# Streaming the 264 token columns of every matmul as two halves in turn, in a one-layer hybrid decoder step

## The chip, the cores and the metric

One Trainium2 chip, one of its cores. The metric is the device time of one execution in microseconds; the time of a kernel is the median of its runs. TensorE (PE) multiplies, with its weight loads shown as an engine of their own (PEld); VectorE (DVE), ScalarE (ACT) and GpSimd (POOL) work on SBUF and PSUM; SyncE (SP) issues most of the DMAs.

## The reference

One step of a decoder layer for 256 prompt tokens and 8 sample tokens, 264 tokens in all, width 2048, all in float32:

```python
def layer(x, ...):
    xn = rmsnorm(x, g_mix)
    z = xn @ w_in                                   # 2048 x 5128
    xr, conv_new = causal_conv(z[..., OFF_RGX:OFF_RGG], conv_buf, conv_w, conv_b)
    ...                                             # RG-LRU over xr, gated by gelu
    y_rg = rmsnorm((h_rg.astype(dt) * jax.nn.gelu(z[..., OFF_RGG:OFF_Q])), g_rg_out)
    ...                                             # q, k, v, gates of the mLSTM
    h_ml, C_new, n_new, m_new = mlstm(q, k, v, logi, logf, C0, n0, m0)
    y_ml = h_ml * jax.nn.sigmoid(z[..., OFF_O:OFF_I])
    x = x + jnp.concatenate([y_rg, y_ml], axis=-1) @ w_out
    xq = (rmsnorm(x, g_xa) @ w_xa_q).reshape(B, L, XA_HEADS, XA_DH)
    ...                                             # softmax attention over 256 memory tokens
    x = x + o @ w_xa_o
    xf = rmsnorm(x, g_ffn)
    x = x + (jax.nn.silu(xf @ w_ffn_gate) * (xf @ w_ffn_up)) @ w_ffn_down
```

The layer ends with a last RMSNorm, and the new states and the memory keys and values are outputs too.

## The kernel before, in words

Activations are held transposed: the model dimension lies on the 128 partitions in 16 chunks (`KC`), and the 264 tokens (`N`; the first 256, `T`, are the prompt, the last 8 the samples) lie along the free dimension. So the weights are the stationary operand of a matmul (128 x 128) and the tokens the moving one (128 x 264).

To keep float32 accuracy in the fast one-pass format `F32R`, both operands are split into a high part and a low part (`HL` holds such pairs in tiles of the pool `B`, four chunks of 264 columns to a tile). `mm3` makes three matmuls of one product, high x high, high x low and low x high, all of which accumulate in one PSUM bank. A projection step (`proj`) does this for all 16 chunks of the model dimension, 48 matmuls, and leaves 128 output channels x 264 tokens in a bank. `pe_if` does the same for the gate columns with two matmuls a chunk.

A table `steps` lists the weight pieces in their order: the combined input projection (41 pieces), the output projection (16), the queries (16), memory keys and values, the attention's output (16), then for three parts of the feed-forward width the gate and up pieces in turn, each followed by the 16 pieces of the down projection. For each step the main loop starts the load of a later piece on SP's queue, lets ACT and DVE split the next piece into its halves (a tile `w`), issues the matmuls, and hands the bank to an evacuation function (`evac_...`, `residual`, `final`) that is emitted one step later. Side work (recurrences, attention, norms) is cut into generators that a pump places between the steps by a price model. Inside this, the Tile scheduler orders instructions by a simulated timeline, and only SP's order is kept as written.

The evacuation functions read the bank from PSUM on DVE (or ACT) with the tokens in order, mostly as `ps[:, :N]`, multiply by the row of inverse norms `rstd` or add to the residual `xres`. Two of them part the prompt columns from the 8 sample columns: `evac_rgx` writes the prompt part into a row with three leading zeros and each sample behind its own three history values, and `evac_q` writes the samples into `qsm`. `final(15)` reads the last output tile in two pieces so that DVE and ACT follow each other sooner.

Matmuls that are not of 264 columns (memory keys and values, attention, sums over tokens, the broadcast of norms) and the plain-float matmuls of the RG gates in `rg_gen` don't go through `mm3` with a 264-column bank.

Line 60 of the profile is the wrapper `Engine`, through which all compute instructions of PE, DVE and ACT are called, so the profile's groups are told apart by tile names: `mm` and `ax` are PSUM banks, `w` split weights, `raw` loaded weights, `B` the general pool, `t` temporaries.

Of the kernel before, what the change touches and what calls it, by code (L numbers as in the profile page):

```python
# [13 lines left out]
AF = mybir.ActivationFunctionType  # L14
OP = mybir.AluOpType
AX = mybir.AxisListType

P = 128
D = 2048
KC = D // P  # L20
T = 256
NS = 8
N = T + NS
# [6 lines left out]
KSCALE = 128.0 ** -0.5  # L30
# [50 lines left out]
def layer_kernel(ctx: ExitStack, tc, xT, memT, vec, wrg, w_in, w_out, w_q, w_k, w_v, w_o,  # L81
# [3 lines left out]
    act, dve, pe = Engine(nc.scalar, price_act), Engine(nc.vector, price_dve), Engine(nc.tensor, price_pe)  # L85
# [18 lines left out]
    def B(shape, dt=F32):  # L104
        return sb.tile(shape, dt, tag="B", bufs=NB, name=nm("B"))

    def tmp(w=N, tag="t"):
        t = sb.tile([P, N], F32, tag=tag, bufs=NT if tag == "t" else NL, name=nm(tag))
        return t[:, :w]
# [109 lines left out]
    class W:  # L219
# [3 lines left out]
        def __call__(self, c, w=P):  # L223
# [5 lines left out]
            o = (c % per) * w  # L229
            return wh[:, o: o + w], wl[:, o: o + w]  # L230

    def mm3(ps, a, b, start, stop):
        ah, al = a
        bh, bl = b
        pe.matmul(ps, ah, bh, start=start, stop=False)
        pe.matmul(ps, ah, bl, start=False, stop=False)
        pe.matmul(ps, al, bh, start=False, stop=stop)
# [20 lines left out]
    def side(g, prio=0):  # L258
        x = Gen(g, prio)
        gens.append(x)  # L260
        gens.sort(key=lambda q: q.prio)
        return x
# [12 lines left out]
    def finish(cond):  # L275

        for _ in range(10000):
            if cond():
                return
            pump(1e12)  # L280
        raise RuntimeError("side work does not end")
# [6 lines left out]
    def bank(tag="mm"):  # L288
        return psm.tile([P, 512], F32, tag=tag, bufs=4, name=nm(tag))
# [16 lines left out]
    def V(name, j=0, w=1):  # L306
        o = _V[name][0] + j
        return vecs[:, o: o + w]
# [52 lines left out]
    def sumsq(acc, x, first):  # L361
        if first:
            return act.activation(acc, x, AF.Square)
        s = tmp(x.shape[-1])
        i = act.activation(s, x, AF.Square)
        dve.tensor_add(acc, acc, s)
        return i
# [29 lines left out]
    rstd = const.tile([P, N], F32, name="rstd")  # L397
# [48 lines left out]
    def evac_rgx(n):  # L446
        def f(ps):
            if n == 0:
                rg["xr"] = Arr(RGB)
            z = B([P, 2, 292])  # L450
            zi = z[:, 0, :]
            dve.memset(zi[:, 0:3], 0.0)
            smp = zi[:, 259:291].rearrange("p (b j) -> p b j", j=4)
            hist = V("cst", n * 24, 24).rearrange("p (b j) -> p b j", j=3)
            act.activation(smp[:, :, 0:3], hist, AF.Copy)
            dve.tensor_mul(zi[:, 3:259], ps[:, :T], rstd[:, :T])
            dve.tensor_mul(smp[:, :, 3:4], ps[:, T:N].rearrange("p (b j) -> p b j", j=1),
                           rstd[:, T:N].rearrange("p (b j) -> p b j", j=1))
            rg["z", n] = z
            rg["zn"] = n + 1  # L460
        return f
# [67 lines left out]
    def evac_rgg(n):  # L529
        def f(ps):  # L530
            z = tmp()
            dve.tensor_mul(z, ps[:, :N], rstd)
            act.activation(z, z, AF.Gelu_apprx_tanh)
            h = rg["h"](n)
            dve.tensor_mul(h, h, z)
            sumsq(acc_rg, h, n == 0)
            if n == RGB - 1:
                st["rgout"] = side(rg_out(), 0)
        return f
# [13 lines left out]
    ml = {}  # L553
# [12 lines left out]
    def pe_if(i):  # L566
        ps = bank()
        for c in range(KC):
            w = splits[i, c // 8][:, c % 8, :]
            xh, xl = rx(c)  # L570
            pe.matmul(ps[:, :N], w, xh, start=c == 0, stop=False)
            pe.matmul(ps[:, :N], w, xl, start=False, stop=c == KC - 1)
        return ps

    def evac_if(ps):
        R = Arr(7)
        ml["R"] = R
        li, u, a, b = (R(j)[0:4] for j in range(4))
        act.activation(a, ps[64:68, :N], AF.Copy)
        act.activation(b, ps[96:100, :N], AF.Copy)  # L580
        dve.tensor_add(li, ps[0:4, :N], a)
        dve.tensor_add(u, ps[32:36, :N], b)
        dve.tensor_mul(li, li, rstd[0:4, :])
        dve.tensor_mul(u, u, rstd[0:4, :])
        dve.tensor_scalar(li, li, V("bi")[0:4], None, op0=OP.add)
        dve.tensor_scalar(u, u, V("bf")[0:4], None, op0=OP.add)
        ml["gates"] = side(ml_gates(), 1)
# [52 lines left out]
    def evac_qk(j):  # L640
        def f(ps):
            if j == 0:
                ml["qk"] = Arr(8)
            if j < 4:
                dve.tensor_mul(ml["qk"](j), ps[:, :N], rstd)
            else:
                dve.scalar_tensor_tensor(ml["qk"](j), ps[:, :N], KSCALE, rstd, op0=OP.mult, op1=OP.mult)
            if j == 7:
                ml["sg"] = side(ml_sample(), 3)
                side(ml_prompt(), 2)  # L650
                side(ml_values(), 2)
                ml["pg"] = side(ml_heads(), 2)
        return f

    def evac_v(j):
        def f(ps):
            if j == 0:
                ml["v"] = Arr(8)
            dve.tensor_mul(ml["v"](j), ps[:, :N], rstd)
            ml["vn"] = j + 1  # L660
        return f

# [193 lines left out]
    def evac_o(j):  # L856
        def f(ps):
            z = tmp()
            dve.tensor_mul(z, ps[:, :N], rstd)
            act.activation(z, z, AF.Sigmoid)  # L860
            if j == 0:
                st["yml"] = HL(8)
            finish(lambda: ml.get("nn", 0) > j // 2)
            dve.tensor_mul(z, z, hT["t"](j))
            split(*st["yml"](j), z, V("g_ml", j))
        return f
# [45 lines left out]
    def residual(m, gname, key, last):  # L912

        def f(ps):
            x = xres[:, m, :]
            dve.tensor_add(x, x, ps[:, :N])
            if key is None:
                return
            if m == 0:
                st[key] = HL(KC)  # L920
            split(*st[key](m), x, V(gname, m))
            sumsq(acc_x, x, m == 0)
            if m == KC - 1:
                st["rstd_" + key] = side(last(), -1)
        return f
# [4 lines left out]
    def final(m):  # L930

        def f(ps):
            x = xres[:, m, :]
            if m == 0:
                st["y"] = Arr(KC)
            if m < KC - 1:
                dve.tensor_add(x, x, ps[:, :N])
                sumsq(acc_x, x, m == 0)
            else:
                warm(3)  # L940
                sq = tmp()
                with tc.high_priority():
                    for lo, hi in ((0, P), (P, N)):
                        dve.tensor_add(x[:, lo:hi], x[:, lo:hi], ps[:, lo:hi])
                        act.activation(sq[:, lo:hi], x[:, lo:hi], AF.Square)
                fin_sums(fin["sum"], sq, False)
            act.activation(st["y"](m), x, AF.Copy, scale=V("g_final", m))
            if m == 0:
                act.activation(warm_act, acc_x[:, 0:1], AF.Sqrt)
            elif m == KC - 2:  # L950
                fin["sum"] = bank("ax")
                fin_sums(fin["sum"], acc_x, True)
            elif m == KC - 1:
                rstd_fin(fin["sum"])
        return f
# [33 lines left out]
    qn = {"n": 0}  # L989
    qsm = const.tile([P, KC, NS], F32, name="qsm")  # L990
# [3 lines left out]
    def evac_q(j):  # L994
        def f(ps):
            if j == 0:
                qn["t"] = Arr(KC, T)
            dve.tensor_mul(qn["t"](j), ps[:, :T], rstd[:, :T])
            dve.tensor_mul(qsm[:, j, :], ps[:, T:N], rstd[:, T:N])
            qn["n"] = j + 1  # L1000
            if j == 3:
                with tc.issue_after(st["split"].ins):
                    act.activation(onesr, ones, AF.Copy)
                st["dk"] = side(dec_k(), 5)
                st["dv"] = side(dec_v(), 4)
        return f
# [233 lines left out]
    fz = {}  # L1240
# [6 lines left out]
    def evac_up(part, j):  # L1247
        def g(ps):
            if j == 0:
                st["a", part] = HL(FPARTS[part])  # L1250
            a, b = tmp(), tmp()
            dve.tensor_mul(a, fz["g"][:, :N], rstd)
            act.activation(a, a, AF.Silu)
            dve.tensor_mul(b, ps[:, :N], rstd)
            dve.tensor_mul(b, b, a)
            h, l = st["a", part](j)
            act.activation(h, b, AF.Copy)
            dve.tensor_sub(l, b, h.bitcast(F32))
        return g
# [39 lines left out]
    for i, (src, cols, pef, evf, need) in enumerate(steps):  # L1299
# [18 lines left out]
        ps = pef(i)  # L1318
# [133 lines left out]
```

## Time and profile before

| | |
|---|---|
| median of 3 runs | 1552.85 us (1552.31 to 1553.53) |
| span of the profiled execution | 1548.1 us |
| granted TensorE clock | 0.997 |
| PE busy | 1533.5 us (99%) |
| DVE busy | 1055.5 us (68%) |
| ACT busy | 784.0 us (51%) |
| HBM traffic over the span | 209 GB/s |

Busy time is the union of an engine's instructions in one profiled execution; a group's row gives line, engine, operation, written and read tiles, shapes and count, then busy time in us, the mean of one in ns, and the idle time of the engine just before such instructions with what ended it. The chain is the work that ended last, followed back through its releasers.

### The profile page before, as it was taken

What the parts mean: (1) busy time and instruction counts of PE and PEld (TensorE: products, weight loads), DVE (VectorE), ACT (ScalarE), POOL (GpSimd) and SP (SyncE); (2) the same over time, 40 slices, a digit from 0 to 9 for tenths busy, and PEclk for the clock granted to TensorE, in tenths of its full rate; (3) what the DMA queues carried; (4) which work ended last, traced back from release to release, by engine and by line L of the source; (5) the groups of instructions that cost most, each with busy time, mean ns of one, the idle gap of its engine ahead of it and who ended that gap; (6) DMA issues with size and microseconds to landing.
All of it is one profiled execution on the core that took longest, in us unless ns stands there. A gap on an engine that the chain in (4) does not pass through costs nothing.

```text
span 1548.1 us, 30188 instructions
## 1 busy us (share of the span) xinstructions
PE 1533.5 (99%) x12098; PEld 1500.4 (97%) x12098; DVE 1055.5 (68%) x2026; ACT 784.0 (51%) x1255; POOL 123.7 (8%) x190
## 2 busy tenths in 40 slices
PE   9999999999999999999999999999999999999997
PEld 9999999999999888899999999999999999999997
DVE  7886888796699989876665555445555545555554
ACT  7565775665455656555444444333444433444463
POOL 0001210000134333310000000000000000000000
PEclk9999999999999999999999999999999999999999
DMA  9556984547789887855555555555555555555563
GB/s 301 187 164 204 309 288 171 193 158 259 251 294 356 320 296 252 309 181 180 187 177 181 186 181 188 181 185 183 183 185 181 186 183 186 180 188 178 163 181 107
DMA packets 99757, 326.01 MB, mean 211 GB/s; under 512 B 10945, under 2 KB 19825, under 8 KB 99617
## 3 DMA queue, kind: packets, MB, share of 16 engines
q1 hardware_dynamic: 83472, 269.57, 52.1%
q0 software_dynamic: 15136, 53.16, 9.7%
q8 instruction: 94, 1.54, 0.4%
q10 hardware_dynamic: 1008, 1.36, 0.3%
q14 instruction: 47, 0.38, 0.1%
HBM read 312.78 MB, written 11.28 MB: 209 GB/s over the span
## 4 chain that ended last, share of the span: by engine, by line
PE 96%; DVE 2%; ACT 1%; DMA 0%; issue 0%; SPq 0%; DVEq 0%; ACTq 0%
PE mm L60 90%; PE ax L60 6%; DVE B L60 1%; ACT B L60 0%; DVE w L60 0%; DMA raw<-w_in 0%; ACT w L60 0%; ACT L60 0%; DVE xres L60 0%; DVE c L60 0%; ACT rstd L60 0%; SPq L1278 0%; DVE acc_x L60 0%; DVEq L1429 0%; ACT t L60 0%
## 5 line engine op out<-in xcount | busy, mean ns | idle before, releaser
L60 PE MATMUL mm<-B,w 128*128 128x264 f32 (+1 forms) x10960 | 1365.3, 285 | 4.1 <-DVE w L60 2.4
L60 PEld LDWEIGHTS mm<-B,w 128*128 128x128 f32 x10960 | 1338.6, 188 | 16.4 <-DVE w L60 2.8
L60 ACT ACTIVATE w<-raw 128x1024 fp32r<-128x1024 f32 (+1 forms) x522 | 537.9, 1031 | 654.6 <-PE mm L60 447.3
L60 DVE TENSOR_TENSOR w<-raw,w 128x1024 fp32r<-128x1024 f32 (+1 forms) x522 | 623.1, 1195 | 357.0 <-ACT w L60 356.0
L60 PE MATMUL mm<-w,B 128*128 128x512 f32 x384 | 91.0, 391 | 0.0
L60 PEld LDWEIGHTS mm<-w,B 128*128 128x128 f32 x384 | 70.7, 188 | 14.3
L60 DVE TENSOR_TENSOR t<-mm,rstd 128x264 f32<-128x264 f32 x104 | 44.8, 431 | 44.2 <-PE mm L60 43.5
L1344 POOL TENSOR_TENSOR B<-B,rstd 128x264 f32<-128x264 f32 x4 | 2.8, 736 | 855.5 <-ACT rstd L60 855.5
L60 DVE TENSOR_TENSOR xres<-xres,mm 128x264 f32<-128x264 f32 (+1 forms) x81 | 34.2, 423 | 38.9 <-PE mm L60 38.9
L60 DVE SCALAR_TENSOR_TENSOR B<-B,dw 128x256 f32<-128x256 f32 x128 | 55.6, 488 | 3.9 <-ACT dw L60 3.9
L60 DVE SCALAR_TENSOR_TENSOR dw<-B,qsm,dw 128x256 f32<-128x256 f32 x96 | 49.6, 525 | 0.4
L60 PE MATMUL ax<-B,B 128*128 128x256 f32 (+3 forms) x288 | 48.1, 308 | 0.0
L60 PEld LDWEIGHTS ax<-B,B 128*128 128x128 f32 x288 | 40.8, 190 | 3.2 <-ACT w L60 0.3
L1031 POOL TENSOR_TENSOR ds<-dw,ds 128x256 fp32r<-128x256 f32 x32 | 34.6, 1085 | 108.1 <-ACT ds L60 108.1
L60 ACT ACTIVATE B<-xres,vecs 128x264 fp32r<-128x264 f32 (+1 forms) x64 | 32.1, 502 | 1.5 <-DVE xres L60 1.0
L60 ACT ACTIVATE t<-xres 128x264 f32<-128x264 f32 (+2 forms) x61 | 24.0, 410 | 15.2 <-DVE xres L60 15.2
L1020 POOL DMA_DIRECT2D B<-kcT x32 | 17.3, 542 | 140.1 <-DVE B L60 131.0
L60 ACT ACTIVATE B<-t 128x264 fp32r<-128x264 f32 (+1 forms) x60 | 24.2, 409 | 4.6 <-DVE t L60 4.3
L60 DVE TENSOR_TENSOR acc_x<-acc_x,t 128x264 f32<-128x264 f32 x59 | 25.1, 426 | 1.0 <-ACT t L60 0.5
L60 DVE SCALAR_TENSOR_TENSOR B<-xres,vecs,B 128x264 fp32r<-128x264 f32 x48 | 23.4, 487 | 3.1 <-ACT B L60 3.1
L60 ACT ACTIVATE t<-t 128x264 f32<-128x264 f32 (+1 forms) x61 | 24.8, 406 | 1.3 <-DVE t L60 1.2
L60 ACT ACTIVATE dw<-B,qsm 128x256 f32<-128x256 f32 x32 | 16.2, 507 | 17.4 <-DVE B L60 10.7
(152 smaller groups left out, 666.9 us busy)
## 6 DMA issues: line engine op xcount, KB each, us to landing
raw<-w_gu SPq DMA_DIRECT2D x176, 512.0 KB, 3.5
raw<-w_d SPq DMA_DIRECT2D x80, 512.0 KB, 3.5
raw<-w_in SPq DMA_DIRECT2D x74, 512.0 KB, 4.6
raw<-w_out SPq DMA_DIRECT2D x32, 512.0 KB, 4.0
B<-kcT POOLq DMA_DIRECT2D x32, 512.0 KB, 8.1
raw<-w_q SPq DMA_DIRECT2D x32, 512.0 KB, 3.7
B<-vcT POOLq DMA_DIRECT2D x32, 512.0 KB, 8.5
raw<-w_k SPq DMA_DIRECT2D x32, 512.0 KB, 6.8
```

The costliest lines, as they stand in the source:

```text
L60: return f(*a, **k)
L1020: pool_e.dma_start(kc, kcT[h, b])
L1031: pool_e.tensor_sub(ws[:, 1], acc, ws[:, 0].bitcast(F32))
L1344: e.tensor_mul(st["y"](c), st["y"](c), r)
```

## The change

Four small views are added. `turn` presents 264 token columns in the order 0, 132, 1, 133, ..., 131, 263, and `mm3` and `pe_if` give it to the matmul as the moving operand. The result is written to PSUM without gaps, so that column 2a + b of the bank now holds token 132 b + a. `by2` only gives the bank's columns the same two dimensions. Where an evacuation reads the bank, `unturn` presents the columns with an even number first and then those with an odd number, which is token order again, and `halves` gives the other operands the matching shape. `mm3` decides by the bank's width: only 264-column banks are streamed in the new order.

```diff
+    def by2(x):
+        return x.rearrange("p (a b) -> p a b", b=2)
+    def turn(x):
+        return x.rearrange("p (b a) -> p a b", b=2)
+    def halves(x):
+        return x.rearrange("p (b a) -> p b a", b=2)
+    def unturn(ps):
+        return ps.rearrange("p (a b) -> p b a", b=2)
     def mm3(ps, a, b, start, stop):
         ah, al = a
         bh, bl = b
+        if ps.shape[-1] == N:
+            ps, bh, bl = by2(ps), turn(bh), turn(bl)
         pe.matmul(ps, ah, bh, start=start, stop=False)
...
 # evac_rgx
-            dve.tensor_mul(zi[:, 3:259], ps[:, :T], rstd[:, :T])
-            dve.tensor_mul(smp[:, :, 3:4], ps[:, T:N].rearrange("p (b j) -> p b j", j=1),
+            p2, m = unturn(ps[:, :N]), N // 2
+            dve.tensor_mul(zi[:, 3: 3 + m], p2[:, 0, :], rstd[:, :m])
+            dve.tensor_mul(zi[:, 3 + m: 259], p2[:, 1, : T - m], rstd[:, m:T])
+            dve.tensor_mul(smp[:, :, 3:4], p2[:, 1, T - m:].rearrange("p (b j) -> p b j", j=1),
...
 # evac_rgg; evac_if, evac_qk, evac_v, evac_o, residual, final and evac_up alike
-            dve.tensor_mul(z, ps[:, :N], rstd)
+            dve.tensor_mul(halves(z), unturn(ps[:, :N]), halves(rstd))
...
 # pe_if
-            pe.matmul(ps[:, :N], w, xh, start=c == 0, stop=False)
-            pe.matmul(ps[:, :N], w, xl, start=False, stop=c == KC - 1)
+            pe.matmul(by2(ps[:, :N]), w, turn(xh), start=c == 0, stop=False)
+            pe.matmul(by2(ps[:, :N]), w, turn(xl), start=False, stop=c == KC - 1)
...
 # final, last output tile
-                    for lo, hi in ((0, P), (P, N)):
-                        dve.tensor_add(x[:, lo:hi], x[:, lo:hi], ps[:, lo:hi])
-                        act.activation(sq[:, lo:hi], x[:, lo:hi], AF.Square)
+                    for b in range(2):
+                        xb = halves(x)[:, b, :]
+                        dve.tensor_add(xb, xb, unturn(ps[:, :N])[:, b, :])
+                        act.activation(halves(sq)[:, b, :], xb, AF.Square)
...
 # evac_q
-            dve.tensor_mul(qn["t"](j), ps[:, :T], rstd[:, :T])
-            dve.tensor_mul(qsm[:, j, :], ps[:, T:N], rstd[:, T:N])
+            p2, m = unturn(ps[:, :N]), N // 2
+            dve.tensor_mul(qn["t"](j)[:, :m], p2[:, 0, :], rstd[:, :m])
+            dve.tensor_mul(qn["t"](j)[:, m:T], p2[:, 1, : T - m], rstd[:, m:T])
+            dve.tensor_mul(qsm[:, j, :], p2[:, 1, T - m:], rstd[:, T:N])
```

The number and the shapes of the matmuls stay. DVE gets 24 instructions more, and the scheduler places some side work elsewhere. On DVE, at the start of the query projection, these rows stand before (a bank `mm` is a query tile, `B_4997` the queries, `w` a weight piece, `dw` a decode score):

```order
617 L60 TENSOR_TENSOR w_5061<-raw_4968,w_5061 128x8x128
618 L60 TENSOR_TENSOR w_5064<-raw_4970,w_5064 128x8x128
619 L60 TENSOR_TENSOR B_4997<-mm_4919,rstd 128x256
620 L60 TENSOR_TENSOR qsm<-mm_4919,rstd 128x8
621 L60 TENSOR_TENSOR B_4997<-mm_5006,rstd 128x256
622 L60 TENSOR_TENSOR qsm<-mm_5006,rstd 128x8
623 L60 TENSOR_TENSOR w_5122<-raw_5055,w_5122 128x8x128
624 L60 SCALAR_TENSOR_TENSOR dw_5245<-B_5243,qsm,dw_5245 128x256
```

And these at the same place of the changed kernel:

```order
628 L60 TENSOR_TENSOR w_5074<-raw_4978,w_5074 128x8x128
629 L60 TENSOR_TENSOR B_5005<-mm_4927,rstd 128x132
630 L60 TENSOR_TENSOR B_5005<-mm_4927,rstd 128x124
631 L60 TENSOR_TENSOR qsm<-mm_4927,rstd 128x8
632 L60 TENSOR_TENSOR B_5005<-mm_5015,rstd 128x132
633 L60 TENSOR_TENSOR B_5005<-mm_5015,rstd 128x124
634 L60 TENSOR_TENSOR qsm<-mm_5015,rstd 128x8
635 L60 TENSOR_TENSOR w_5133<-raw_5064,w_5133 128x8x128
636 L60 SCALAR_TENSOR_TENSOR dw_5257<-B_5255,qsm,dw_5257 128x256
```

Each query tile is read from its bank in three pieces instead of two, at the same place among the weight pieces. At the end of the run DVE has before:

```order
1613 L60 TENSOR_TENSOR acc_x<-acc_x,t_17739 128x264
1614 L60 TENSOR_TENSOR xres<-xres,mm_17747 128x128
1615 L60 TENSOR_TENSOR xres<-xres,mm_17747 128x136
1616 L60 TENSOR_SCALAR c_17797<-ax_17743 128x3
1617 L60 RECIPROCAL c_17798<-c_17798 128x3
```

and in the changed kernel:

```order
1632 L60 TENSOR_TENSOR acc_x<-acc_x,t_17763 128x264
1633 L60 TENSOR_TENSOR xres<-xres,mm_17771 128x132 x2
1634 L60 TENSOR_SCALAR c_17821<-ax_17767 128x3
1635 L60 RECIPROCAL c_17822<-c_17822 128x3
1636 L60 TENSOR_TENSOR c_17823<-c_17822 128x3
```

The two pieces of the last output tile are now equal, and nothing else moves there.

More of the change, by code (lines that the diff above doesn't have):

```diff
@@ L578, in evac_if @@
         li, u, a, b = (R(j)[0:4] for j in range(4))
[L579 to L582, printed above, removed]
+        act.activation(halves(a), unturn(ps[64:68, :N]), AF.Copy)
+        act.activation(halves(b), unturn(ps[96:100, :N]), AF.Copy)
+        dve.tensor_add(halves(li), unturn(ps[0:4, :N]), halves(a))
+        dve.tensor_add(halves(u), unturn(ps[32:36, :N]), halves(b))
         dve.tensor_mul(li, li, rstd[0:4, :])
@@ L644, in f @@
             if j < 4:
-                dve.tensor_mul(ml["qk"](j), ps[:, :N], rstd)
+                dve.tensor_mul(halves(ml["qk"](j)), unturn(ps[:, :N]), halves(rstd))
             else:
-                dve.scalar_tensor_tensor(ml["qk"](j), ps[:, :N], KSCALE, rstd, op0=OP.mult, op1=OP.mult)
+                dve.scalar_tensor_tensor(halves(ml["qk"](j)), unturn(ps[:, :N]), KSCALE, halves(rstd),
+                                         op0=OP.mult, op1=OP.mult)
             if j == 7:
@@ L658, in f @@
                 ml["v"] = Arr(8)
-            dve.tensor_mul(ml["v"](j), ps[:, :N], rstd)
+            dve.tensor_mul(halves(ml["v"](j)), unturn(ps[:, :N]), halves(rstd))
             ml["vn"] = j + 1
@@ L858, in f @@
             z = tmp()
-            dve.tensor_mul(z, ps[:, :N], rstd)
+            dve.tensor_mul(halves(z), unturn(ps[:, :N]), halves(rstd))
             act.activation(z, z, AF.Sigmoid)
@@ L915, in f @@
             x = xres[:, m, :]
-            dve.tensor_add(x, x, ps[:, :N])
+            dve.tensor_add(halves(x), halves(x), unturn(ps[:, :N]))
             if key is None:
@@ L936, in f @@
             if m < KC - 1:
-                dve.tensor_add(x, x, ps[:, :N])
+                dve.tensor_add(halves(x), halves(x), unturn(ps[:, :N]))
                 sumsq(acc_x, x, m == 0)
@@ L1251, in g @@
             a, b = tmp(), tmp()
-            dve.tensor_mul(a, fz["g"][:, :N], rstd)
+            dve.tensor_mul(halves(a), unturn(fz["g"][:, :N]), halves(rstd))
             act.activation(a, a, AF.Silu)
-            dve.tensor_mul(b, ps[:, :N], rstd)
+            dve.tensor_mul(halves(b), unturn(ps[:, :N]), halves(rstd))
             dve.tensor_mul(b, b, a)
```

## The prediction

> **What bounds the kernel now.** I read the cores view first (clock), then the page's shares and its chain, then the groups by form for TensorE, then the chain in order of time, which gives stretches of like matmuls with their count.
>
> ```profile
> core 0: 1548.1 us, clock 0.997
> ```
> ```profile
> PE 1533.5 (99%) x12098; PEld 1500.4 (97%) x12098; DVE 1055.5 (68%) x2026; ACT 784.0 (51%) x1255; POOL 123.7 (8%) x190
> PE 96%; DVE 2%; ACT 1%; DMA 0%; issue 0%; SPq 0%; DVEq 0%; ACTq 0%
> L60 PEld LDWEIGHTS mm<-B,w 128*128 128x128 f32 x10960 | 1338.6, 188 | 16.4 <-DVE w L60 2.8
> ```
> TensorE is busy for 99% of the span at a granted clock of 0.997, and 96% of the chain is PE. Nothing else is near the bound. Which matmuls these are is told by the groups by form (count, then union of busy time and the modelled mean of one; the mean overlaps with its neighbours and is not a spacing):
>
> ```profile
> L60 PE MATMUL mm<-B,w 128*128 128x264 f32 x10448 | 1272.4, 283 | 4.1 <-DVE w L60 2.4 <-DVE B L60 1.7
> L60 PE MATMUL mm<-w,B 128*128 128x512 f32 x384 | 91.0, 391 | 0.0
> L60 PE MATMUL ax<-B,w 128*128 128x264 f32 x144 | 22.2, 284 | 0.7 <-ACT w L60 0.7
> L60 PE MATMUL ax<-B,B 128*128 128x264 f32 x32 | 8.4, 386 | 0.0
> ```
> The change touches the first and the third row: 10448 + 144 = 10592 matmuls of 264 columns in the fast float format. The fourth row is 16 plain-float matmuls (two records each), which the change leaves alone. For 10448 matmuls PE idled 4.1 us, so their spacing is set by TensorE itself. The spacings come from the chain in order of time (start, length, count):
>
> ```profile
> 95.12 0.89 PE ax L60 x4
> 228.80 9.94 PE mm L60 x82
> 415.30 5.76 PE mm L60 x48
> 498.52 5.69 PE mm L60 x25
> 788.03 746.34 PE mm L60 x6232
> ```
> In the long last stretch a 264-column matmul takes 746.34/6232 = 119.8 ns; at 415 us it takes 120.0 ns, at 229 us 121.2 ns. The row at 498.52 is 25 matmuls of 512 columns: 227.6 ns each. The row at 95.12 is four plain-float records of 264 columns: 222.5 ns each. So 248 more columns cost 227.6 - 119.8 = 107.8 ns, that is 0.435 ns a column (an estimate from two rows), 114.8 ns for 264 columns, and 5.0 ns of the 119.8 are left as a fixed part. The bound is the rate at which TensorE takes token columns out of SBUF.
>
> **The change part by part.** Nothing is removed: the matmuls, their weights, their count and their outputs' places in PSUM are as before. Three things differ.
>
> *First, the read of the tokens.* Each of the 10592 matmuls now takes column 0, column 132, column 1, column 133 and so on. Neighbours in time lie 132 words (528 bytes) apart instead of one word. Every nanosecond that this adds to or takes from one matmul is 10.6 us of the total, all of it on the path, because PE is 99% busy and waits for nothing. No row of the trace shows a matmul whose moving operand is read with a step, so the price must be bounded. Below: at best the fixed 5.0 ns go (if they are collisions of token reads with weight loads that the new order avoids): 10592 x 5.0 = 53 us gained. Above: if the stream gets one column in the time of two, the nearest row is the plain-float record, where TensorE takes 222.5 ns for 264 columns, twice as long a column. That is +102.7 ns, 10592 x 102.7 = +1088 us; doubling the column part and keeping the fixed part gives 2 x 114.8 + 5.0 = 234.6 ns, +114.8 ns, +1216 us. If a step costs four column times, 4 x 114.8 = 459 ns, +3595 us. I take the plain-float row, 222.5 ns. My reason is that at 0.435 ns a column TensorE reads faster than any other engine in this trace, and does so with words that are neighbours; the DVE row below has 1.04 ns a column. A stream at this rate most plausibly lives on one access to SBUF that yields several neighbouring words. With the new order each such access would yield one word that is used at once. Whether the reader can keep two such accesses open in turn is what no row says.
>
> [...]
>
> *Second, the evacuations.* DVE and ACT now read PSUM with a step of two words. The nearest rows are the same reads without the step:
>
> ```profile
> L60 DVE TENSOR_TENSOR t<-mm,rstd 128x264 f32<-128x264 f32 x104 | 44.8, 431 | 44.2 <-PE mm L60 43.5 <-issue 0.2
> L60 DVE TENSOR_TENSOR xres<-xres,mm 128x264 f32<-128x264 f32 x79 | 33.7, 427 | 35.3 <-PE mm L60 35.3
> L60 DVE TENSOR_TENSOR B<-mm,rstd 128x256 f32<-128x256 f32 x21 | 8.7, 414 | 1.3 <-PE mm L60 1.2
> L60 DVE TENSOR_TENSOR xres<-xres,mm 128x128 f32<-128x128 f32 x1 | 0.3, 286 | 3.6 <-PE mm L60 3.6
> ```
> From 128 to 264 columns the add into the residual goes from 286 to 427 ns: 1.04 ns a column and 153 ns fixed. If a step of two doubles the column part, an evacuation gets 274 ns longer; for some 225 of them that is 62 us of DVE time. If it costs nothing, zero. I take zero to 62 us, none of it on the path: DVE is busy for 68% of the span and would be at 72%.
>
> *Third, the split evacuations.* Eight of the RG input columns and the sixteen queries are now evacuated in three pieces (132, 124, 8) instead of two (256, 8): 24 more instructions at 153 ns, 3.7 us of DVE. Both meet where DVE is fullest beside these matmuls, the query projection; the steady part stands below it:
>
> ```profile
> 380.00:475.00 95.00, 95.00 (x794) 95.00 (x793) 79.42 (x201) 49.05 (x76) 21.46 (x32) 1.00 0.80 290
> 900.00:1000.00 100.00, 100.00 (x837) 100.00 (x836) 54.86 (x64) 40.27 (x46) 0.00 (x0) 1.00 0.55 185
> ```
> These are rows of the windows view: length, then busy time of PE, PEld, DVE, ACT, POOL. Sixteen queries at 0.15 + 0.27 us add 6.8 us to 79.4 of 95 us, which still fits; the cover is the time DVE spends waiting for ACT and for PE. If that cover were gone, 7 us at most would show, as a late PSUM bank or a late weight piece (the weight splits queue behind the evacuations on DVE). At the end of the run the two pieces of the last output tile are 132 and 132 columns instead of 128 and 136:
>
> ```profile
> 1535.44 0.49 DVE L60 TENSOR_TENSOR xres<-xres,mm 128x128 f32<-128x128 f32 x2 [3.64 <-PE mm L60]
> ```
> They are on the path, and a doubled PSUM read would cost 0.27 us there; I count zero.
>
> The sum, with 222.5 ns: 1548.1 us of span + 1088 = 2636 us. The median of the runs, 1552.85, is 4.75 us above the span of the profiled execution; keeping that distance gives 2641 us. What would be late next is still PE: the work beside it (DVE 1055.5 us, DMA about half of the span) fits into the longer span with more room than before.
>
> **The rivals.**
>
> *Faster, by calmer reads.* The fixed 5.0 ns and the spread between 119.8 and 121.2 ns in matmuls of one shape say that something other than the column count takes a little time. If that is token reads and weight loads meeting in SBUF, and streaming two places in turn avoids it, the spacing falls to between 114.8 and 119.8 ns: 1500 to 1553 us, 1526 us in the middle. It decides as soon as a matmul gains 0.3 ns. For it: weight loads run under the stream nearly always (PEld busy for 97%). Against: there are only 5 ns to win, and the gain needs the rate a column to hold under the step.
>
> *Slower, by collisions with the weight loads.* The step itself is free, but the stream visits two places and hits the concurrent weight load more often. The price of a lost cover is a load's own slot:
>
> ```profile
> 1534.09 0.76 PEld L60 LDWEIGHTS ax<-ones,acc_x 128*128 128x128 f32 x6
> ```
> Six loads in 0.76 us, the last one modelled at 188 ns: (760 - 188)/5 = 114 ns a load. Half of that uncovered is +57 ns, about +604 us, 2157 us; between a tenth and nine tenths it is 1670 to 2640 us. It would show as a spacing between 120 and 220 ns that differs from stretch to stretch.
>
> *Four column times.* 459 ns a matmul, 5148 us. Against it: even the plain-float format, with its several passes, is at 222.5 ns a record.
>
> *Nothing.* If TensorE fetches each column for itself, the neighbours don't matter, and the kernel is at 1553 us, up to 1560 us if the 7 us of the query projection show.
>
> **How the numbers follow.** Half rate 0.46, collisions 0.20, four column times 0.08, nothing 0.05, faster 0.21. A measurement of this kernel tells about 0.2% (3.1 us) from no change, and the cases above lie well outside of it except the fourth. So slower 0.46 + 0.20 + 0.08 = 0.74, the same 0.05, faster 0.21. The time is that of the likeliest case, 2641 us; its own range is 2560 to 2770 us, from a spacing a little under the plain-float row to the 234.6 ns. The range for 8 in 10 has to take in cases of both signs: it begins at 1520 us, which leaves out the better part of the faster case (about 0.09), and ends at 2770 us, which leaves out the four column times (0.08).
>
> **What would show it.** In the profile after, the last long stretch of the chain gives the spacing directly: 222 to 235 ns for 6232 matmuls says half rate; 115 to 119 says calmer reads; a value that differs between stretches says collisions. The 512-column stretch near the middle must keep 227.6 ns, since its reads are as before, and the plain-float records their 222.5 ns. The evacuation rows t<-mm and xres<-mm show the price of the step in PSUM by their means (431 and 427 ns before; 705 and 700 if the column part doubles). PE must stay at 99%; if it drops, or its idle time before the 264-column group grows beyond some 10 us, an evacuation has come onto the path and my second step was wrong. I am wrong altogether if the spacing stays within a few ns of 119.8.

## The result, and the profile after

The changed kernel takes 1483.28 us (median of 4 runs, 1479.40 to 1485.04) against 1552.58 us (4 runs): a ratio of 0.9551, 95% interval 0.9535 to 0.9568. It is faster by 4.5%, where 2641 us was forecast, and it lies outside the stated range too.

The cores view and the page's shares and chain of the changed kernel:

```profile
core 0: 1482.9 us, clock 0.993
PE 1461.7 (99%) x12098; PEld 1426.8 (96%) x12098; DVE 1054.2 (71%) x2050; ACT 785.6 (53%) x1257; POOL 125.1 (8%) x190
PE 92%; DVE 3%; ACT 2%; DMA 2%; issue 1%; POOL 0%; DVEq 0%; SPq 0%; ACTq 0%
```

TensorE still sets the end, with the same number of instructions in 71.8 us less busy time. Where the gain comes from stands in the groups by form (count, then busy time and modelled mean, then idle time before) and in the chain in order of time:

```profile
L60 PE MATMUL mm<-B,w 128*128 128x264 f32 x10448 | 1199.5, 277 | 8.5 <-DVE w L60 4.6 <-DVE B L60 2.0 <-ACT w L60 1.9
L60 PE MATMUL mm<-w,B 128*128 128x512 f32 x384 | 91.5, 392 | 0.0
L60 PE MATMUL ax<-B,B 128*128 128x264 f32 x32 | 8.4, 386 | 0.0
```
```profile
60.67 0.89 PE ax L60 x4
256.98 55.68 PE mm L60 x494
405.49 5.40 PE mm L60 x48
768.31 701.20 PE mm L60 x6232
```

The long last stretch falls from 746.34 to 701.20 us for the same 6232 matmuls: 112.5 ns each instead of 119.8. The granted clock is 1.00 in this stretch before and after, so the gain is not one of the clock. The 48 matmuls at 405 us take 112.5 ns as well (120.0 before). The 512-column matmuls and the plain-float records, which the change leaves alone, keep their busy times nearly or wholly (91.5 us against 91.0, and 8.4 us).

10592 matmuls at 7.24 ns would give 76.7 us; the span fell by 65.2 us. (The medians differ by 69.3 us: a run's time is some 2 us above its span, so the profiled execution of the kernel before was a quick one, and that of the changed kernel, with 1485.04 us, the slowest of its four.) Of the missing 11.5 us, 11.0 are lost before 257 us. The row of 494 matmuls starts at 256.98 us; before, it starts here:

```profile
258.49 59.28 PE mm L60 x494
```

Up to there the chain has gained 1.5 us, while the 1731 matmuls of 264 columns that the trace has ahead of it (counted in the kernel before) had 12.5 us to give. The windows view of 100 to 200 us (length; busy time and count of PE, PEld, DVE, ACT, POOL; granted clock) shows where most of them go, for the kernel before, the run e1 below that has the new evacuations without the new stream, and the changed kernel:

```profile
100.00:200.00 100.00, 98.47 (x756) 94.66 (x756) 76.76 (x224) 68.92 (x156) 18.22 (x34) 0.98 0.74 241
```
```profile
100.00:200.00 100.00, 97.19 (x737) 93.42 (x736) 75.24 (x219) 71.46 (x153) 17.74 (x33) 0.97 0.73 238
```
```profile
100.00:200.00 100.00, 94.28 (x720) 89.69 (x719) 74.47 (x215) 69.41 (x155) 18.23 (x34) 0.93 0.73 239
```

TensorE stands still for 5.7 us here after the change, against 1.5 us before, and the granted clock is 0.93 against 0.98; over 100 us that is some 5 us more (an estimate). The run e1 lies between, with 2.8 us and 0.97. The chain before leaves TensorE once in this stretch, from 101.83 to 121.52 us. The chain after leaves it there too, with one table load of ACT more (`ACT_TABLE_LOAD`, the rows `ACT L60` of 1.28 us; the whole run has 14 instead of 12), and then a second time, from 136.11 to 166.97 us, over ACT, DVE and a round trip through DRAM (`scr`) that is not on the chain before or in e1.

```profile
101.83 1.06 ACT w L60
103.64 1.28 ACT L60
112.63 1.28 ACT L60
114.38 3.14 DVE B L60 x9
121.52 15.76 PE mm L60 x116
137.28 1.36 PE ax L60 x13
138.64 5.76 PE mm L60 x48
```
```profile
99.34 1.04 ACT w L60
100.41 1.28 ACT L60
102.57 1.28 ACT L60
111.44 1.28 ACT L60
113.19 3.14 DVE B L60 x9
120.33 15.78 PE mm L60 x116
138.12 4.07 DMA scr<-lt
143.04 7.37 DMA B<-scr
166.97 2.93 PE ax L60 x8
```

The first fence is the chain before, the second after. The serial work of gates and recurrence keeps its length (the nine DVE pieces take 3.14 us in both), and the faster matmuls reach the place where they need its results sooner and wait. The 116 matmuls behind the first wait take 15.78 us, no less than before (15.76 us; 136 ns each in both): the granted clock during them is 0.84, against 0.89 before, which eats the gain (an estimate from spacings and clocks: 112.5/0.84 and 119.8/0.89 ns are both about 134 ns).

### The profile page after: what moved, and what is told of

It reads as the page before. It is cut to its first block, busy times and chain, and to the rows that moved or that the text cites. A ratio compares the mean times of both kernels' runs of the same rounds, so it can differ in the third digit from the quotient of the medians.

```text
span 1482.9 us, 30202 instructions
## 1 busy us (share of the span) xinstructions
PE 1461.7 (99%) x12098; PEld 1426.8 (96%) x12098; DVE 1054.2 (71%) x2050; ACT 785.6 (53%) x1257; POOL 125.1 (8%) x190
## 4 chain that ended last, share of the span: by engine, by line
PE 92%; DVE 3%; ACT 2%; DMA 2%; issue 1%; POOL 0%; DVEq 0%; SPq 0%; ACTq 0%
PE mm L60 88%; PE ax L60 4%; DVE B L60 2%; DVE w L60 1%; DMA raw<-w_in 1%; ACT B L60 1%; ACT w L60 1%; DMA B<-scr 0%; DMA scr<-lt 0%; ACT L60 0%; DVE t L60 0%; DVE acc_x L60 0%; ACT t L60 0%; DVE c L60 0%; DVE xres L60 0%
## 5 line engine op out<-in xcount | busy, mean ns | idle before, releaser
L60 PE MATMUL mm<-B,w 128*128 128x264 f32 (+1 forms) x10960 | 1292.5, 280 | 8.5 <-DVE w L60 4.6
L60 PEld LDWEIGHTS mm<-B,w 128*128 128x128 f32 x10960 | 1266.2, 190 | 21.5 <-DVE w L60 5.4
L60 DVE TENSOR_TENSOR w<-raw,w 128x1024 fp32r<-128x1024 f32 (+1 forms) x522 | 625.6, 1200 | 319.2 <-ACT w L60 318.5
L60 ACT ACTIVATE w<-raw 128x1024 fp32r<-128x1024 f32 (+1 forms) x522 | 536.1, 1029 | 573.9 <-PE mm L60 394.0
L60 PE MATMUL mm<-w,B 128*128 128x512 f32 x384 | 91.5, 392 | 0.0
L60 PEld LDWEIGHTS mm<-w,B 128*128 128x128 f32 x384 | 70.4, 188 | 14.3
L60 DVE TENSOR_TENSOR t<-mm,rstd 128x264 f32<-128x264 f32 x104 | 44.9, 433 | 29.4 <-PE mm L60 29.4
L60 DVE SCALAR_TENSOR_TENSOR B<-B,dw 128x256 f32<-128x256 f32 x128 | 52.4, 464 | 2.7 <-ACT dw L60 2.5
L60 DVE TENSOR_TENSOR xres<-xres,mm 128x264 f32<-128x264 f32 (+1 forms) x81 | 34.3, 424 | 28.0 <-PE mm L60 27.8
L60 PE MATMUL ax<-B,B 128*128 128x256 f32 (+3 forms) x288 | 49.8, 314 | 1.4 <-DVE B L60 1.4
L60 DVE SCALAR_TENSOR_TENSOR dw<-B,qsm,dw 128x256 f32<-128x256 f32 x96 | 49.2, 520 | 0.7
L60 PEld LDWEIGHTS ax<-B,B 128*128 128x128 f32 x288 | 41.7, 194 | 5.1 <-DVE B L60 2.0
L60 ACT ACTIVATE B<-xres,vecs 128x264 fp32r<-128x264 f32 (+1 forms) x64 | 32.1, 501 | 2.5 <-DVE xres L60 2.0
L60 ACT ACTIVATE t<-xres 128x264 f32<-128x264 f32 (+1 forms) x61 | 23.9, 408 | 15.9 <-DVE xres L60 15.9
L60 DVE TENSOR_TENSOR acc_x<-acc_x,t 128x264 f32<-128x264 f32 x59 | 25.3, 429 | 1.0 <-ACT t L60 0.5
L60 DVE SCALAR_TENSOR_TENSOR B<-xres,vecs,B 128x264 fp32r<-128x264 f32 x48 | 23.5, 490 | 3.1 <-ACT B L60 3.1
L60 ACT ACTIVATE t<-t 128x264 f32<-128x264 f32 (+1 forms) x61 | 24.9, 408 | 1.3 <-DVE t L60 1.2
L60 ACT ACTIVATE t<-B,B 128x128 f32<-128x128 f32 x64 | 21.6, 390 | 7.3 <-DMA B<-scr 7.3
L60 ACT ACTIVATE B<-t 128x264 fp32r<-128x264 f32 (+1 forms) x60 | 24.0, 409 | 0.4 <-DVE t L60 0.3
```

Source lines behind the costliest of these rows:

```text
L60: return f(*a, **k)
```

## The experiments

In the runs e2, e5, e6, e8 to e10 and e12 to e14 only the views `turn` and `by2` differ from the changed kernel (in e1 `turn` alone): `turn` sets the order in which the tokens are streamed, `by2` has the same shape for PSUM; the excerpts show the line of `turn` alone. The spacing is read from the chain's last long stretch of matmuls. From 1300 to 1400 us the granted clock is 1.00 in the kernel before, the changed kernel, e1, e2, e5, e8 and e12 to e14; over the whole run it is 0.992 (e4) to 0.997 (e7, e9) in e3, e4, e6, e7, e9 and e10. Runs e2 to e14 are single executions.

**e1_evac_only: the stored order, with the new evacuations.**

```diff
     def turn(x):
-        return x.rearrange("p (b a) -> p a b", b=2)
+        return x.rearrange("p (a b) -> p a b", b=2)
```


> The changed kernel with the tokens streamed in their stored order again; the evacuations keep the stepped reads of PSUM and the 24 extra pieces, so the token order of the results is not restored. Theory A (the stored order collides in SBUF with the weight load that runs under the stream) and theory B (reading neighbouring words one after the other is slow by itself) both say that the spacing of 264-column matmuls is back at 119.8 ns in the long last stretch, and the time at 1553 to 1565 us: whatever it is above 1552.6 is what evacuations and moved side work cost. Theory C (the gain is not in the stream but in the evacuations and what the scheduler moved) says about 1483 us with 119.8 ns not seen again.

```profile
793.29 746.34 PE mm L60 x6232
```
1555.22 us, ratio 1.0017 (1.0008 to 1.0026): the old spacing, to the hundredth of a microsecond over 6232 matmuls. The whole gain is in the stream (theory C falls), and the evacuations with what they move cost 2.6 us (1.2 to 4.0 us by the interval). The chain loses them before its row of 494 matmuls: from there to the last stretch it takes 529.7 us, against 529.5 us before. The query projection, where the prediction looked for such a cost, lies behind that row and shows none.

**e2_step4: no neighbours at all.**

```diff
-        return x.rearrange("p (b a) -> p a b", b=2)
+        return x.rearrange("p (a b) -> p b a", b=4)
```


> The changed kernel, but the tokens are streamed with a step of four words (16 bytes): 0, 4, 8, ..., 260, then 1, 5, ..., so that no access has a neighbour among the accesses around it. The token order of the results is not restored. The step of the prediction that failed said that a stream without neighbours halves: about 222 ns a matmul, 2640 us. If two places in turn were only saved because both accesses stay open, this run must show it: 222 ns. Theory B says 112.5 ns and 1483 us, since no neighbours follow each other. Theory A leaves it open between 112.5 and 125 ns, as the stream meets the weight load in another pattern.

```profile
1307.89 252.62 PE mm L60 x1051
```
2823.15 us, 240.4 ns a matmul. The stream does halve, as the prediction said of a stream without neighbours, and by more than its 222.5 ns. Theory B, that neighbours one after the other are what is slow, falls.

**e3_before_wo0 and e4_after_wo0: weights elsewhere.** In the kernel before and in the changed one:

```diff
-    WO, WW = 48, 8 * N + 64
+    WO, WW = 0, 8 * N + 64
```


> The kernel before with the split weights 48 words lower in their tile (offset 0 instead of 48), so that weights and tokens stand 48 words closer in their addresses. Theory A says that the spacing of 264-column matmuls moves off 119.8 ns by some ns (115 to 135), the time by 10.6 us for each ns. Theory B says that it stays at 119.8 ns, and 1553 us within 0.3%.

> The changed kernel with the same 48 words less. Theory A says that the spacing stays at 112.5 ns if streaming two places in turn avoids the weight load wherever it is, or rises above it by some ns if 48 was a lucky distance. Theory B says 112.5 ns and 1483 us.

```profile
795.72 756.65 PE mm L60 x6232
```
```profile
768.66 701.20 PE mm L60 x6232
```
With the stored order the spacing rises to 121.4 ns (1567.85 us). With the halves it doesn't move at all (701.20 us again; 1485.40 us). So the 7 ns of the stored order depend a little on where the weights lie, and the halves don't feel this one other place. That spoke for theory A.

**e7_one_weight: a weight load that stands still** (in the kernel before).

```diff
+        if ps.shape[-1] == N:
+            ah, al = (w[:, 0:1].to_broadcast([P, P]) for w in (ah, al))
```


> The kernel before, tokens in their stored order, but each weight load of a 264-column matmul in the triple products reads the first of its 128 weight columns 128 times instead of all of them (so all output channels of a matmul come out alike). The load has as many columns, but stands on one word of SBUF. Theory A (the stored order loses its 7 ns to collisions with the moving weight load): the spacing falls from 119.8 ns to near 112.5 ns, the time to about 1480 us, or it becomes very different from matmul to matmul where that one word is in the way. Theory B (the stored order is slow by itself): 119.8 ns, 1553 us.

```profile
792.31 749.73 PE mm L60 x6232
```
1557.51 us, 120.3 ns: no gain. Loads that stand on one word of SBUF, instead of running through 128, leave the 7 ns in place. Where the weights are read moves the loss by a nanosecond or two, but the running of the loads through SBUF doesn't make it.

**e5_step4_halves, e6_quarters and e8_step2.**

```diff
 # e5
+        return x.rearrange("p (b c d) -> p d c b", b=2, d=4)
 # e6
+        return x.rearrange("p (b a) -> p a b", b=4)
 # e8
+        return x.rearrange("p (a b) -> p b a", b=2)
```


> The changed kernel with the tokens streamed as 0, 132, 4, 136, 8, 140, ..., 128, 260, then 1, 133, 5, ...: two halves in turn as in the change, but within a half with the step of four words of the run before, so that no 16 bytes are touched twice within a short time. The token order of the results is not restored. Theory D (what halves the rate is that a 16-byte piece of SBUF is used once and then dropped; the two halves in turn are fast because two pieces stay open and each is used four times): 240 ns a matmul, 2823 us. Theory E (two accesses that follow each other may go anywhere as long as they don't hit the same part of SBUF; 16 bytes apart is the same part, 528 bytes apart is not): 112.5 ns, 1483 us.

> The changed kernel with four quarters in turn: 0, 66, 132, 198, 1, 67, ... The token order of the results is not restored. Theory D with two open pieces only: 240 ns and 2823 us; with four or more open pieces 112.5 ns and 1483 us. Theory E: 112.5 ns unless 264 bytes apart is the same part of SBUF, then 240 ns.

> The changed kernel with the tokens streamed with a step of two words: 0, 2, 4, ..., 262, then 1, 3, ... The token order of the results is not restored. Two accesses in a row fall into the same 16 bytes, then the next 16 bytes follow. [...] If the rate of the step of four grows with the distance, some 180 ns and 2190 us.

```profile
1300.16 251.46 PE mm L60 x1051
```
```profile
884.89 888.20 PE mm L60 x6232
```
```profile
1295.25 1483.53 PE mm L60 x6232
```
239.3 ns (2807.74 us), 142.5 ns (1788.74 us) and 238.0 ns (2795.63 us). Distance alone doesn't save a stream (theory E falls with e5). The surprise is e8: a step of two uses each of theory D's pieces of 16 bytes twice in a row and still takes 238.0 ns, about twice the 119.8 ns of the stored order. Pieces of two words (8 bytes) would explain it; the quarters fit nothing yet.

**e9_pairs and e10_distance66.**

```diff
 # e9
+        return x.rearrange("p (b a c) -> p a b c", b=2, c=2)
 # e10
+        return x.rearrange("p (h b a) -> p h a b", b=2, h=2)
```


> The changed kernel with pairs in turn: 0, 1, 132, 133, 2, 3, 134, 135, ... The token order of the results is not restored. The runs so far say that TensorE gets the tokens in pieces of two words, about one piece in 0.9 ns: the stored order and the halves need 132 pieces, a step of two or four needs 264. Theory F1 (pieces that follow each other closely in SBUF are fetched a little slower than pieces from two places in turn): 112.5 ns, about 1483 us. Theory F2 (what helps is that a piece's second word is used two columns later, so that two fetches are followed by two columns that need none; the place is of no matter): each piece is used up at once, 119.8 ns, about 1555 us.

> The changed kernel with halves in turn inside each half: 0, 66, 1, 67, ..., 65, 131, then 132, 198, ..., so that the two places are 264 bytes apart instead of 528. The token order of the results is not restored. Theory F2: 112.5 ns, 1483 us. Theory F1: 112.5 ns if 264 bytes is far enough, otherwise up to 119.8 ns. If the four quarters were slow because of the distance of 66 words and not because of their number, this run is slow as well: 142 ns, 1790 us.

```profile
1004.02 1059.15 PE mm L60 x6232
```
```profile
764.57 701.20 PE mm L60 x6232
```
Pairs in turn take 170.0 ns (2078.88 us), which neither theory allowed; halves 264 bytes apart take 112.5 ns (1481.34 us). Pairs use up each piece of two words at once, so pieces of two words can't be the unit. What fits is to count the columns at even and at odd positions of the stream apart (theory G, stated with e12 below). In the halves the even columns read tokens 0, 1, 2, 3 and the odd ones 132, 133, 134, 135: each takes four words of a 16-byte piece in a row. In the stored order the even columns read 0, 2, 4, 6, two words of each piece; with a step of two or four it is one.

**e12_step2_halves, e13_apart4 and e14_apart2** test that count.

```diff
 # e12
+        return x.rearrange("p (b c d) -> p d c b", b=2, d=2)
 # e13
+        return x.rearrange("p (h b a) -> p h a b", b=2, a=4)
 # e14
+        return x.rearrange("p (h b a) -> p h a b", b=2, a=2)
```


> The changed kernel with two halves in turn and a step of two in each: 0, 132, 2, 134, 4, 136, ..., then 1, 133, 3, ... The token order of the results is not restored. Theory G (TensorE takes the columns with even number and those with odd number through two readers, each of which holds one piece of 16 bytes, and a piece must be used at least twice in a row by its reader to keep the rate): each reader uses a piece twice, so about 112.5 to 120 ns, 1483 to 1560 us; 112.5 ns if the 7 ns of the stored order come from both readers wanting the same piece, 119.8 ns if they come from only two uses a piece. Theory D (one reader, pieces of two words, one fetch in 0.9 ns): 264 fetches, 239 ns, 2800 us.

> The changed kernel with the two places only four words apart: 0, 4, 1, 5, 2, 6, 3, 7, then 8, 12, 9, 13, ... The token order of the results is not restored. Theory G: the even columns use a 16-byte piece four times in a row, the odd ones the next piece, and they never share one: 112.5 ns, 1483 us. If the two places have to be far apart, 119.8 ns or more.

> The changed kernel with the two places two words apart: 0, 2, 1, 3, then 4, 6, 5, 7, ... The token order of the results is not restored. Theory G: both readers want the same 16-byte piece at the same time and use it twice each, as in the stored order: 119.8 ns, 1555 us. A theory in which any two places in turn help says 112.5 ns; theory D, with each piece of two words used in two steps, 112.5 to 120 ns.

```profile
795.59 749.77 PE mm L60 x6232
```
```profile
768.36 701.20 PE mm L60 x6232
```
```profile
792.52 746.34 PE mm L60 x6232
```
120.3 ns (1560.92 us), 112.5 ns (1485.09 us), 119.8 ns (1554.42 us). All three come out as theory G has it, and e12 excludes pieces of two words (239 ns). They also tell what the 7 ns go with: in e12 even and odd columns are far apart and share nothing, yet with two uses a piece the loss is there; in e13 they are neighbours and it is gone with four uses. And e14 has an order as nested as e13's at the old spacing, so the shape of the view alone gains nothing. The orders together, by the uses of a 16-byte piece that even and odd columns make in a row:

| order of the columns | uses | ns a matmul |
|---|---|---|
| halves; halves 66 words apart (e10); 4 words apart (e13) | 4 | 112.5 |
| stored (before, e1); 2 words apart (e14) | 2 | 119.8 |
| halves with a step of two (e12) | 2 | 120.3 |
| quarters (e6) | 4, but in turn with a second piece | 142.5 |
| pairs (e9) | 2, but in turn with a second piece | 170.0 |
| step of two (e8), step of four with and without halves (e5, e2) | 1 | 238.0 to 240.4 |

Two readers, one for even and one for odd columns, is the reading that fits these; it is inferred from times, not seen. So counted, the piece has 16 bytes: with 8 bytes the stored order and the step of two would both use a piece once, but take 119.8 and 238.0 ns; with 32 bytes the stored order and e13 would both use it four times, but take 119.8 and 112.5 ns. Open is why quarters and pairs, whose readers change their piece at every use, lose only part of the rate.

**b_pieces, b_both and b_turnkv: a better version.** The same order for the memory keys and values, whose matmuls the change left alone (`b_turnkv`); two pieces instead of three in the split evacuations (`b_pieces`); both.

```diff
 # b_turnkv: pe_v, and pe_k alike; evacuations through unturn
-                    pe.matmul(ps, mh[:, s], wh, start=(kc == 0), stop=False)
+                    ps, th, tl = by2(ps), turn(wh), turn(wl)
+                    pe.matmul(ps, mh[:, s], th, start=(kc == 0), stop=False)
...
 # b_pieces: evac_rgx, and evac_q alike
-            dve.tensor_mul(zi[:, 3: 3 + m], p2[:, 0, :], rstd[:, :m])
-            dve.tensor_mul(zi[:, 3 + m: 259], p2[:, 1, : T - m], rstd[:, m:T])
+            dve.tensor_mul(halves(zi[:, 3: 3 + N]), unturn(ps[:, :N]), halves(rstd))
```


> The changed kernel, with two things more. The 512-column and 256-column matmuls of the memory keys and values are streamed as halves in turn too (256 and 128 words apart), with evacuations that restore the order. And the two evacuations that the change cut into three pieces go back to two: one of 264 columns that runs over the prompt's end into words that are written right after, and one of the 8 samples. If halves in turn work at these distances, 512 columns fall from 227 to about 216 ns and 256 columns from 118 to about 109 ns: 640 x 11 + 472 x 9 = 11 us where TensorE sets the pace; with 2 to 3 us for the pieces 1469 to 1475 us. If the two places hit the same part of SBUF when they are a power of two apart, the same matmuls get slower, up to twice: 640 x 227 ns + 472 x 118 ns = 200 us more.

> The changed kernel with the second part of the kernel before alone: evacuations of the RG input and the queries in two pieces instead of three, matmuls as in the changed kernel. The run with the stored order said that evacuations and moved side work cost 2.6 us. If that is the 24 pieces, this gives 1480 us (ratio to the kernel before 0.953); if it is the read of PSUM with a step, or another place of side work, it stays at 1483 us (0.955).

> The changed kernel, with the matmuls of the memory keys and values streamed as halves in turn as well, and the evacuations of the change as they are (three pieces). In the two runs before, the two pieces alone gave nothing (1485.5 us) and both things together 1473.7 us. So 1470 to 1474 us, ratio 0.949 to 0.952, if the gain is that of the matmuls; 1476 us or more if the pieces had a part in it.

The pieces alone give nothing: 1485.49 us, 0.9569 (0.9553 to 0.9585). Both: 1473.73 us, 0.9510 (0.9494 to 0.9526). The keys and values alone: 1472.03 us, 0.9494 (0.9480 to 0.9507), the lowest median here, though its interval overlaps with that of both. A stretch of 25 matmuls of 512 columns in the chain of the changed kernel and of `b_turnkv`:

```profile
545.14 5.74 PE mm L60 x25
```
```profile
538.53 5.40 PE mm L60 x25
```
229.6 ns falls to 216.0 ns. The places are 1024 bytes apart there, so the distance may be a power of two. Had the 2.6 us of e1 been the number of pieces, `b_pieces` would be at a ratio of about 0.953, outside its interval; that makes it unlikely, no more, as side work lies elsewhere in that run too (its chain runs over DVE between 418 and 446 us, where that of the changed kernel stays on TensorE). The two table loads more that both e1 and `b_pieces` have (2.6 us of ACT together) may be the cause; no run takes them away alone.

## Why the prediction was wrong

- **What bounds the kernel** was right: TensorE's stream, at 119.8 ns a matmul, and each nanosecond was worth 9.0 us of the span (65.2 us for 7.24 ns), against 10.6 us in the prediction; the last stretch gave its full share (45.1 us for 6232 matmuls).
- **The step that failed** is the price of the read: "With the new order each such access would yield one word that is used at once." It put the spacing at 222.5 ns; the runs showed 112.5 ns. It took neighbours in time over the whole stream for what counts. The general part holds, near the 234.6 ns of the prediction's second bound (a stream whose even and odd columns each use a 16-byte piece once takes 238.0 to 240.4 ns), but the change is not such a stream: counted for even and odd columns apart, it raises the uses of a piece from two to four. The prediction named the question, whether two accesses can stay open in turn, and then answered it by the nearest row instead of leaving it open; 0.74 for slower was too much on a question that no row bore on.
- **The most that could be gained** was mis-sized. The 0.435 ns a column came from 512- and 264-column matmuls that both lost time in the stored order. With halves the two rows are 216.0 and 112.5 ns: 0.417 ns a column and 2.3 ns fixed. So 7.2 ns could be won, not 5.0, and the lower end of the faster case lay at about 1476 us, not 1500. The range began at 1520 us by choice and left out most of that case; the time came out there, below even its 1500 us. (The 4.75 us that the sum sets between span and median join two different executions; in one and the same it is some 2 us. That changes nothing here.)
- **The faster rival** (0.21) had the right sign and the wrong cause: e7 shows that the loss stays when the loads no longer run through SBUF, and in e12 and e13 it follows the uses of a piece. A stream without any loads beside it wasn't tried, so a share of the loads in the 7 ns isn't excluded; what removes them is the order. The rival of more collisions with the loads (0.20) has no support: the halves keep 112.5 ns with the weights elsewhere (e4).
- **The evacuations** came out at the lower bound: the reads of PSUM with a step of two words cost next to nothing, as the first two rows of the changed kernel show against 431 and 427 ns. The third is one of the new pieces.

```profile
L60 DVE TENSOR_TENSOR t<-mm,rstd 128x264 f32<-128x264 f32 x104 | 44.9, 433 | 29.4 <-PE mm L60 29.4
L60 DVE TENSOR_TENSOR xres<-xres,mm 128x264 f32<-128x264 f32 x79 | 33.8, 428 | 24.6 <-PE mm L60 24.4
L60 DVE TENSOR_TENSOR B<-mm,rstd 128x132 f32<-128x132 f32 x21 | 6.1, 290 | 0.5 <-PE mm L60 0.3
```
- **What would be late next** was said to be PE still. For the faster case this was not worked out, and there it is wrong between 100 and 200 us, where the waits for side work and the lower clock take about 9 us of the gain back (the stretch from 96 to 189 us got 4.7 us longer, while its 577 matmuls of 264 columns had 4.2 us to give).

## What to carry to other kernels

When no row of a profile shows the access that a change brings in, say that the sign is open, and look for what the new pattern is to the reader, not to the eye; here one run with another order would have told more than any argument from rows. A fast-format matmul whose moving operand lies in stored order may leave 6% of TensorE's time unused though it is "99% busy" (119.8 against 112.5 ns here): try two places in turn, which costs little where the results are read out of PSUM anyway (2.6 us of 1553 here). Look for the serial stretch that will not shrink before counting a gain over the whole span.

## What the hardware showed that was not expected

- The spacing of fast-format matmuls of 264 columns went with the uses in a row of a 16-byte piece by even and by odd columns: 112.5 ns at four, 119.8 to 120.3 at two, 238.0 to 240.4 at one.
- Two places in turn work 16 (e13), 264 (e10), 528 (the change) and 1024 bytes apart (`b_turnkv`) alike: 112.5 ns for 264 columns at the first three, 216.0 ns for 512 columns at the last.
- The spacing in the stored order depends on where the weights lie (119.8 against 121.4 ns for 48 words); with four uses a piece it doesn't (112.5 ns at both places).
- The granted clock was lower right after the wait of TensorE near 120 us. In the changed kernel TensorE is busy for 2.8 of the 6 us from 114 to 120 us, at a clock of 0.88; the clock is 0.50 in the next 4 us, 0.83 in the 4 us after, and then 1.00 again.
- DVE reads PSUM with a step of two words at the rate of neighbouring words (433 against 431 ns).
